# A two-layer hybrid trunk on one core: single returns of gated outputs, the place of one gate tile, and rotary tables one group later

## The chip, the cores and the metric

The kernel runs on one core of a Trainium2 chip, in one launch. The metric is the device time of that launch in microseconds (us). "Before" was run three times: 1938.21 us in the median (1937.47 to 1940.67). One further run carried the hardware profiler; its time and trace are what the text below reads.

In the profile PE is TensorE's matrix multiplications and PEld its weight loads, DVE is VectorE, ACT is ScalarE, POOL is GpSimd, and SP is SyncE, which in this kernel issues nearly all DMA transfers. L126 is line 126 of the kernel.

## The reference

A sequence of 512 positions of width 2048 passes two layers; everything is float32.

```python
def pool_mixer_layer(x, norm_g, w_in, w_group, scale, w_out):     # layer A
    h = rmsnorm(x, norm_g)
    proj = h @ w_in                                               # 2048 -> 2 * 4096
    u, gate = proj[..., :W_A], proj[..., W_A:]
    u = u.reshape(B, S, N_POOL_GROUPS, G_A)                       # 4 groups of 1024
    pooled = jnp.stack([causal_mean_pool(u[:, :, gi], w) - u[:, :, gi]
                        for gi, w in enumerate(POOL_WINDOWS)], axis=2)   # 2, 4, 8, 16
    y = jnp.einsum('bsgc,gcd->bsgd', pooled, w_group).reshape(B, S, W_A) * scale
    return x + (y * jax.nn.silu(gate)) @ w_out                    # 4096 -> 2048
...
# layer B: 16 heads; a key has 128 plain and 64 rotary columns, a value 128
k, v = shared_kv(x, ...)            # latent of 512 -> keys (QK-norm, rotary) and values
h = rmsnorm(x, norm_g)
proj = h @ w_in                     # q latent of 512, and 16 gate tiles of 128
q = qk_norm_rope(rmsnorm(latent) @ w_q_b, ...)
o = chunk_causal_attention(q, k, v) # query blocks of 128, mask by chunks of 64
x = x + (o * jax.nn.silu(gate)) @ w_out
```

The rotation uses cos and sin of position times frequency, tables that both keys and queries of layer B need.

## The kernel before, in words

**Products.** Activations stand with channels on the 128 partitions and the 512 positions along the row. For precision each operand is split in two parts, hi (a cast, on ACT) and lo (the rest, on DVE), and a product is three matmuls: hi·hi (L144), hi·lo (L145), lo·hi (L146), in `mm3`. `split` (L149) makes the two parts of an activation. `load_w` does the same for a weight tile: a DMA into `raw` (three buffers), the cast into `whi` (L126), the subtraction into `wlo` (L127) (four buffers each). `proj` walks over a weight in tiles of four 128-row slices, of 256 KB each.

**Layer A.** The in-projection (lines up to L412) leaves its 64 output tiles in DRAM. Then four groups g follow, one for each pooling window. In each, eight `y_tile`s fetch a gate tile z from DRAM (L453), multiply by the norm (L454), apply SiLU (L455), make the group product with weights `awg` and combine it with z (L458) and split it. Then 16 output products with weights `awo` follow, and with every second one of them the next group's `pooled_tile` loads a tile from DRAM and pools it (`pool_tile`, lines L232 to L259; its first step on DVE is L243, the window sums L250). `rope_tables` (L181 to L206, small DVE operations and two sines on ACT) stands in the code between the y tiles and the output products of group 0. `rope_gains` (L208 to L218), which multiplies the tables by the norm gains, is written further down, where they are used; the scheduler starts it early, behind the tables.

**Layer B, the gate tiles.** After the latents, `gate_unit` computes gate tiles 0 to 13 and stores each in DRAM (`gates`, named `gd` in the trace). Tiles 14 and 15 are made by `gate_part`, in four pieces of 12 matmuls each, within the first round of attention below.

**Attention.** The heads go in eight rounds hg of two heads. TensorE's order is written out by hand and pinned. A main sequence of 64 steps (hg, head h, query block i) issues scores (`score_unit`, L786; on DVE a memset L787, the maximum L789, its scaling L791), the exponential on ACT (`exp_unit`, L799), the scaling on DVE (`scale_unit`, L805 and L806), the transposition (`pt_unit`, L814, with splits L826 and L828) and the product with values (`pv_unit`, L844 to L846). Beside it a list `fill` of small pieces is used up between these steps by `fill_to`: a piece is a planned time, a weight tile, a function and its arguments. `prep_items(hg)` builds a round's pieces: k and v (`kv_part`, 16 pieces, L641 to L643), q (`q_part`, 16 pieces, L664 to L666), transpositions (`tr_unit`, L752) and statistics. The pieces of round 0 run ahead of the steps; those of a later round run between the steps of the round ahead of it, and the tail between those of round 7. `split_due` issues the load of a weight tile four tiles ahead of its use. Other engines than PE are ordered by a scheduler that takes the written order and a simulated time line.

**The return of the gated outputs.** A head's attention output is multiplied by its gate and stored in DRAM (L849, L852). For the last product, over 16 heads with weights `bwo`, it comes back: `og_load(h)` (L916) loads it into a buffer `at` (heads 0 to 7) or `bt` (8 to 13), `og_unit(h)` splits it there (L149). Heads 14 and 15 never leave the chip. `part(o, k0, n)` is a fill piece: n heads from k0 on, into output tile o, one `bwo` tile. The fill's end, `tail`, holds the parts of output tiles 0 to 2 for heads 0 to 13, with `ld` (loads) and `og` (splits) between. After the main sequence `out_unit` does the same for tiles 3 and 4 (`NO` is 3), then all five get heads 14 and 15, and the other eleven tiles follow whole; `out_store` (L936 to L940) adds the residual and stores.

Of the kernel before, what the change touches and what calls it, by code (L numbers as in the profile page):

```python
# [47 lines left out]
def trunk_kernel(  # L48
# [417 lines left out]
    for g in range(NG):  # L466
        ys = []
        for o in range(8):
            with ExitStack() as c5:
# [4 lines left out]
                ys.append(y_tile(g, o, pooled))  # L474
        if g == 0:
            rope_tables()
# [317 lines left out]
    def exp_unit(hg, h, i):  # L794
        n = (i + 1) * P
        s, nm, rq = st[hg][("P", h, i)]
        pe = tt_()
        sm = small(1, "sm", 4)
        A.activation(pe[:, 0:n], s[:, 0:n], AF.Exp, bias=nm, scale=rq, accum_out=sm)  # L799
        st[hg][("P", h, i)] = pe, sm  # L800

    def scale_unit(hg, h, i):
        pe, sm = st[hg][("P", h, i)]
        n = (i + 1) * P
        V.reciprocal(sm, sm)  # L805
        V.tensor_scalar(pe[:, 0:n], pe[:, 0:n], sm, None, ALU.mult)  # L806

# [46 lines left out]
    def prep_items(hg, nxt, mid=()):  # L854


        def piece(us, fn, *a, w=None):
            return us, w, fn, a
# [19 lines left out]
        first += mid  # L878
        if end:
            first += ld(0, 1, 2, 3)  # L880
        first += [q(0, 0), q(0, 1), kq(3), q(0, 2), q(0, 3)]
        if own:
            first += [piece(0, kstats_unit, hg)]
        first += [q(1, 0), q(1, 1), qq(0), q(1, 2), q(1, 3)]
        if own:
            first += [kr(0), tr_(0)]
        first += [q(2, 0), qq(1), q(2, 1)]
        if own:
            first += [kr(1)]
        if end:  # L890
            first += og(0)
        first += [q(2, 2), q(2, 3)]
        if own:
            first += [tr_(2, 0)]
        if end:
            first += og(1) + ld(4, 5)
        first += [q(3, 0), qq(2), q(3, 1)]
        if end:
            first += og(2) + ld(6, 7)
        first += [q(3, 2), q(3, 3)]  # L900
        if end:
            first += og(3)
        first += nxt[:1] + [qq(3)]
        if own:
# [63 lines left out]
    def ld(*hs):  # L968
        return [(0, None, og_load, (h,)) for h in hs]
# [7 lines left out]
    tail = (part(0, 0, 4) + part(1, 0, 4) + og(4, 5) + part(2, 0, 4) + og(6, 7) + ld(8, 9) + part(0, 4, 4) +  # L977
            ld(10, 11) + part(1, 4, 4) + og(8) + part(2, 4, 4) + og(9, 10) + ld(12, 13) + og(11) +
            part(0, 8, 4) + part(1, 8, 4) + og(12) + part(2, 8, 4) + og(13) +
            part(0, 12, 2) + part(1, 12, 2) + part(2, 12, 2))  # L980
# [71 lines left out]
    for m in range(len(seq) + 2):  # L1052
        now = seq[m] if m < len(seq) else None
        if now:
# [4 lines left out]
            score_unit(*now)  # L1059
            beside(hg, 4 * h + i, 0)  # L1060
        if m >= 2 and seq[m - 2][2] % 2:
            pv_unit(*seq[m - 2][:2], seq[m - 2][2] // 2)
        if now:
            fill_to(at_ + share * 0.35)
            exp_unit(*now)
        if 1 <= m <= len(seq):
            pt_unit(*seq[m - 1])
        if now:
# [3 lines left out]
            fill_to(at_ + share)  # L1072
    fill_to(c + 99)
    PINNED = (mybir.EngineType.PE,)
# [81 lines left out]
```

## Time and profile before

| | before |
|---|---|
| median of 3 runs | 1938.21 us (1937.47 to 1940.67) |
| profiled execution | 1935.33 us |
| its span in the trace | 1933.4 us |
| granted TensorE clock | 1.0 |
| PE busy | 1910.7 us, 99%, 11356 instructions |
| DVE busy | 1279.4 us, 66% |
| ACT busy | 806.7 us, 42% |
| POOL busy | 287.3 us, 15% |
| DMA | 251.26 MB, mean 130 GB/s |

The span runs from the first to the last instruction in the trace; the 1.9 us between it and the execution's time lie outside. The "chain that ended last" is followed back from the last instruction, at each step to what released it; a row of it has start, length (us) and what ran. "issue" in it is time for which the trace shows no cause. A row of waits names the engine and line that waited, the instruction that ended the wait, the total, the number of waits and the longest. In a row of a timeline stand start, length, engine, line, operation, output, inputs and shape, and in brackets the idle time before it with what ended it.

### The profile page before, as it was taken

How to read it: one execution, taken by the hardware profiler on the slowest of the kernel's cores; microseconds unless marked ns; L12 is line 12 of the kernel's file. 1: busy time of each engine (PE TensorE's matmuls, PEld its weight loads, DVE VectorE, ACT ScalarE, POOL GpSimd, SP SyncE). 2: the span in 40 equal slices, each digit the busy share in tenths (PEclk: the TensorE clock that was granted, in tenths of full speed). 3: DMA queues.
4: the chain of work that ended last, by engine and by line, in shares of the span. 5: the costliest groups of instructions: out<-in, count | busy, mean ns of one | idle time of the engine just before them, and what ended most of it. 6: DMA issues, size and time to landing. Idle time of an engine off the chain costs nothing.

```text
span 1933.4 us, 30664 instructions
## 1 busy us (share of the span) xinstructions
PE 1910.7 (99%) x11356; PEld 1704.1 (88%) x11356; DVE 1279.4 (66%) x2249; ACT 806.7 (42%) x1506; POOL 287.3 (15%) x436
## 2 busy tenths in 40 slices
PE   8999999999999999999999999999999999999999
PEld 8999999999999977888888888888888999988887
DVE  8677786797666677486595477474335888896332
ACT  8444333333333433233333354233235777774221
POOL 0433232343323100000000000000001332320000
PEclk9999999999999999999999999999999999999999
DMA  6555443434444446434344344233432222243642
GB/s 190 160 157 164 143 141 122 131 121 143 156 134 137 157 138 213 128 122 143 120 123 137 107 147 134 91 100 118 124 111 89 87 90 81 78 137 111 211 120 88
DMA packets 176646, 251.26 MB, mean 130 GB/s; under 512 B 15728, under 2 KB 95984, under 8 KB 176496
## 3 DMA queue, kind: packets, MB, share of 16 engines
q1 hardware_dynamic: 176208, 249.10, 41.1%
q8 instruction: 89, 1.46, 0.3%
q14 instruction: 61, 0.50, 0.1%
q10 hardware_dynamic: 288, 0.20, 0.0%
HBM read 216.21 MB, written 33.03 MB: 129 GB/s over the span
## 4 chain that ended last, share of the span: by engine, by line
PE 88%; DMA 4%; DVE 4%; issue 1%; ACT 1%; SPq 1%; POOL 0%; DVEq 0%; ACTq 0%; POOLq 0%
PE mm L146 15%; PE mm L144 14%; PE mm L145 14%; PE k L337 10%; PE k L335 10%; PE k L333 10%; PE sc L786 2%; PE mm L641 2%; PE mm L643 1%; PE mm L642 1%; PE mm L664 1%; PE mm L666 1%; PE mm L665 1%; PE tr L814 1%; PE tr L752 1%
## 5 line engine op out<-in xcount | busy, mean ns | idle before, releaser
L126 ACT CAST whi<-raw 128x512 fp32r<-128x512 f32 (+2 forms) x421 | 254.4, 609 | 515.7 <-PE mm L145 444.4
L333 PE MATMUL k<-xc,hi 128*128 128x256 f32 x1680 | 460.1, 283 | 0.1
L335 PE MATMUL k<-xc,hi 128*128 128x256 f32 x1680 | 460.0, 283 | 0.0
L127 DVE TENSOR_TENSOR wlo<-raw,whi 128x512 fp32r<-128x512 f32 (+2 forms) x421 | 285.0, 678 | 237.7 <-ACT whi L126 236.5
L337 PE MATMUL k<-xc,lo 128*128 128x256 f32 x1680 | 417.8, 283 | 1.1 <-DVE lo L315 1.0
L146 PE MATMUL mm<-bt,wlo 128*128 128x512 f32 x944 | 368.5, 391 | 1.7 <-DVE wlo L127 1.7
L144 PE MATMUL mm<-bt,whi 128*128 128x512 f32 x944 | 367.9, 390 | 0.9 <-ACT bt L149 0.9
L145 PE MATMUL mm<-bt,whi 128*128 128x512 f32 x944 | 367.2, 389 | 0.0
L314 ACT CAST hi<-raw 128x1792 fp32r<-128x1792 f32 x120 | 202.8, 1690 | 364.5 <-PE k L337 249.9
L315 DVE TENSOR_TENSOR lo<-raw,hi 128x1792 fp32r<-128x1792 f32 x120 | 248.4, 2070 | 158.9 <-ACT hi L314 158.7
L333 PEld LDWEIGHTS k<-xc,hi 128*128 128x128 f32 x1680 | 322.5, 192 | 0.3 <-ACT hi L314 0.3
L335 PEld LDWEIGHTS k<-xc,hi 128*128 128x128 f32 x1680 | 322.5, 192 | 0.0
L337 PEld LDWEIGHTS k<-xc,lo 128*128 128x128 f32 x1680 | 296.8, 192 | 2.2 <-DVE lo L315 1.7
L146 PEld LDWEIGHTS mm<-bt,wlo 128*128 128x128 f32 x944 | 177.2, 188 | 40.4 <-DVE wlo L127 3.1
L144 PEld LDWEIGHTS mm<-bt,whi 128*128 128x128 f32 x944 | 177.2, 188 | 38.0 <-ACT bt L149 1.3
L145 PEld LDWEIGHTS mm<-bt,whi 128*128 128x128 f32 x944 | 177.2, 188 | 37.0 <-DVE bt L149 0.2
L146 PE MATMUL mm<-at,wlo 128*128 128x512 f32 x432 | 168.6, 390 | 1.7 <-DVE wlo L127 1.7
L145 PE MATMUL mm<-at,whi 128*128 128x512 f32 x432 | 168.9, 391 | 0.2 <-DVE at L149 0.2
L144 PE MATMUL mm<-at,whi 128*128 128x512 f32 x432 | 168.5, 390 | 0.0
L310 POOL TENSOR_TENSOR raw<-raw 128x256 f32<-128x256 f32 x120 | 97.1, 809 | 434.4 <-DVE raw L308 412.2
L311 POOL TENSOR_TENSOR raw<-raw 128x256 f32<-128x256 f32 x120 | 105.7, 880 | 9.2
L146 PEld LDWEIGHTS mm<-at,wlo 128*128 128x128 f32 x432 | 81.1, 188 | 20.0 <-DVE wlo L127 3.2
(1151 smaller groups left out, 2541.7 us busy)
## 6 DMA issues: line engine op xcount, KB each, us to landing
raw<-awin SPq DMA_DIRECT2D x240, 256.0 KB, 3.2
raw<-awo SPq DMA_DIRECT2D x128, 256.0 KB, 2.9
raw<-bwin SPq DMA_DIRECT2D x80, 256.0 KB, 2.8
raw<-awg SPq DMA_DIRECT2D x64, 256.0 KB, 2.8
raw<-bwo SPq DMA_DIRECT2D x59, 256.0 KB, 2.8
scr<-e SPq DMA_DIRECT2D x56, 256.0 KB, 2.7
raw<-wkvb SPq DMA_DIRECT2D x32, 256.0 KB, 2.9
raw<-wqb SPq DMA_DIRECT2D x32, 192.0 KB, 2.4
```

Source lines behind the costliest of these rows:

```text
L126: A.copy(hi[:, :n], raw[:, :n])
L127: V.tensor_tensor(lo[:, :n], raw[:, :n], f(hi[:, :n]), ALU.subtract)
L144: T.matmul(dst, wh, xh, start=first, stop=False)
L145: T.matmul(dst, wh, xl, start=False, stop=False)
L146: T.matmul(dst, wl, xh, start=False, stop=last)
L310: G.tensor_tensor(c[:, :, 6, :], c[:, :, 4, :], c[:, :, 2, :], ALU.add)
L311: G.tensor_tensor(c[:, :, 7, :], c[:, :, 6, :], c[:, :, 3, :], ALU.add)
L314: A.copy(hi, c[:, :, 1:8, :])
L315: V.tensor_tensor(lo, c[:, :, 1:8, :], f(hi), ALU.subtract)
L333: T.matmul(dst, hi[:, j % 2, wi, :], xh[j][:, xi, :], start=first, stop=False, skip_group_check=True)
L335: T.matmul(dst, hi[:, j % 2, wi, :], xl[j][:, xi, :], start=False, stop=False, skip_group_check=True)
L337: T.matmul(dst, lo[:, j % 2, wi, :], xh[j][:, xi, :], start=False, stop=last, skip_group_check=True)
```

## The change

Five edits.

1. The rotary tables are written behind group 1's y tiles instead of group 0's.
2. Gate tile 15 leaves its place between kv and q of round 0 (gate 14 stays there). Its four pieces go behind q, ahead of round 1's kv, with round 0's last transpositions and the q statistics among and behind them.
3. Among round 7's pieces the gated outputs come back one at a time: `ld(0)` to `ld(3)` are spread over the q pieces. And `og_unit` gets an order: its cast on ACT stands behind the last exponential that is written ahead of it, its subtraction on DVE behind the last scaling.
4. In the tail the first four heads' parts are cut into two halves of two heads, with one `og` and one `ld` between each; loads and splits run some pieces ahead of their use.
5. Output tile 3's four products for heads 0 to 13 are written around the last scores and the last value products, inside the pinned order. Tile 4's stay behind.

```diff
-        if g == 0:
+        if g == 1:
             rope_tables()
...
-        A.activation(pe[:, 0:n], s[:, 0:n], AF.Exp, bias=nm, scale=rq, accum_out=sm)
+        st["exp"] = A.activation(pe[:, 0:n], s[:, 0:n], AF.Exp, bias=nm, scale=rq, accum_out=sm)
...
-        V.tensor_scalar(pe[:, 0:n], pe[:, 0:n], sm, None, ALU.mult)
+        st["scale"] = V.tensor_scalar(pe[:, 0:n], pe[:, 0:n], sm, None, ALU.mult)
...
-        if end:
-            first += ld(0, 1, 2, 3)
...
+        if end:
+            first += ld(0)
         first += [q(1, 0), q(1, 1), qq(0), q(1, 2), q(1, 3)]
...
+        if end:
+            first += ld(1)
         first += [q(2, 0), qq(1), q(2, 1)]
...
         if end:
-            first += og(0)
-        first += [q(2, 2), q(2, 3)]
+            first += og(0) + ld(2)
+        first += [q(2, 2), q(2, 3), q(3, 0), qq(2), q(3, 1)]
+        if end:
+            first += og(1) + ld(3)
+        first += [q(3, 2), q(3, 3)]
         if own:
-            first += [tr_(2, 0)]
...
-            return first + [piece(0, qstats_unit, hg), tr_(3)] + nxt[1:4] + [tr_(5)] + nxt[4:]
-        return first + nxt[1:]
+            return (first + nxt[:1] + [tr_(3)] + nxt[1:4] + [tr_(2, 0), qq(3), piece(0, qstats_unit, hg)] +
+                    nxt[4:5] + [tr_(5)] + nxt[5:])
+        return first + nxt[:1] + [qq(3)] + nxt[1:]
...
-        split(f(lo) if h < 14 else gated[h], hi, lo)
+
+        for ins, name in zip(split(f(lo) if h < 14 else gated[h], hi, lo), ("exp", "scale")):
+            if name in st:
+                tc.add_manual_dep(ins.ins, st[name].ins.name, mybir.DependencyInfo(
+                    mybir.DependencyClass.NoSync, mybir.DependencyReason.DATA), reason="softmax first")
...
-    tail = (part(0, 0, 4) + part(1, 0, 4) + og(4, 5) + part(2, 0, 4) + og(6, 7) + ld(8, 9) + part(0, 4, 4) +
...
+    tail = (part(0, 0, 2) + og(2) + ld(4) + part(1, 0, 2) + og(3) + ld(5) + part(2, 0, 2) + og(4) +
+            part(0, 2, 2) + ld(6) + og(5) + part(1, 2, 2) + ld(7) + og(6) + part(2, 2, 2) + ld(8, 9) + og(7) +
+            part(0, 4, 4) + og(8) + ld(10, 11) + og(9) + part(1, 4, 4) + og(10) + ld(12, 13) + og(11) +
+            part(2, 4, 4) + part(0, 8, 4) + og(12) + part(1, 8, 4) + og(13) + part(2, 8, 4) +
...
-    fill = prep_items(0, fill, gate_items(14) + gate_items(15))
+    fill = prep_items(0, gate_items(15) + fill, gate_items(14))
...
+        if m == len(seq) + 1:
+            out_unit(NO, 4, 4)
         if m >= 2 and seq[m - 2][2] % 2:
             pv_unit(*seq[m - 2][:2], seq[m - 2][2] // 2)
...
+        if m == len(seq):
+            fill_to(c + 99)
+            out_unit(NO, 0, 4)
...
-    fill_to(c + 99)
+    out_unit(NO, 8, 4)
+    out_unit(NO, 12, 2)
...
-    for o in range(NO, NO + 2):
-        for k0, n in ((0, 4), (4, 4), (8, 4), (12, 2)):
-            out_unit(o, k0, n)
+    for k0, n in ((0, 4), (4, 4), (8, 4), (12, 2)):
+        out_unit(NO + 1, k0, n)
```

How this stands in the engines' order, at three places. On ACT in round 6, where round 7's pieces stand between the steps, around head 12's second query block (tt__18109 is its exponential), before: three casts of gated outputs (`at<-at`) stand in a row, then one, then two more right behind an exponential (L799).

```order
L126 CAST whi<-raw 128x384
L149 CAST at<-at 128x512 x3
L149 CAST at<-mm 128x256
L826 CAST xt<-tr 128x128
L126 CAST whi<-raw 128x384
L149 CAST at<-at 128x512
L149 CAST bt<-tr 128x512
L799 ACTIVATE tt__18109,sm<-sc,nm,qy 128x256
L149 CAST at<-at 128x512 x2
```

On the same engine now, a little later in that round (tt__18246 and tt__18323 are exponentials of the next steps):

```order
L826 CAST xt<-tr 128x2x128
L826 CAST xt<-tr 128x128
L799 ACTIVATE tt__18246,sm<-sc,nm,qy 128x512
L149 CAST at<-at 128x512
L670 COPY qt<-mm 128x384
L126 CAST whi<-raw 128x256
L677 ACTIVATE junk,ssq<-qt 128x192 x2
L126 CAST whi<-raw 128x256
L826 CAST xt<-tr 128x2x128 x2
L799 ACTIVATE tt__18323,sm<-sc,nm,qy 128x128
L149 CAST at<-at 128x512
```

Each such cast stands alone, and behind an exponential. The weights' casts of 256 columns are those of the half parts.

On DVE, in group 1's output stage, the difference (a piece of it; tt__9144 is group 2's first pooled tile, tt__8012 a pooled tile of the same kind in group 0's output stage, qsin a table with gains):

```order
+L199 SCALAR_TENSOR_TENSOR tt__9043<-tt__9043 128x128 x2
+L200 SCALAR_TENSOR_TENSOR tt__9043<-tt__9043 128x128
 L127 TENSOR_TENSOR wlo<-raw,whi 128x512
 L204 SCALAR_TENSOR_TENSOR cn<-cn,sn 128x128
 L205 SCALAR_TENSOR_TENSOR sn<-sn 128x128
 L217 SCALAR_TENSOR_TENSOR qsin<-cn,cs 128x32
-L243 SCALAR_TENSOR_TENSOR tt__8012<-tt__8010,r 128x512
+L243 SCALAR_TENSOR_TENSOR tt__9144<-tt__9142,r 128x512
 L218 TENSOR_TENSOR qsin<-cn,cs 128x32
```

The tables stand around a pooled tile of group 1's output stage as they stood around one of group 0's.

On SP, in round 0 of the attention, the difference (bwin are gate weights, wqb those of q, wkvb those of kv; tt__14259 is gate tile 15):

```order
 L606 DMA gd<-tt__14055 128x512
-L125 DMA raw<-bwin 128x512 x5
+L125 DMA raw<-bwin 128x512
+L125 DMA raw<-wqb 128x384 x4
+L125 DMA raw<-bwin 128x512 x3
+L953 DMA gd<-tt__14259 128x512
+L125 DMA raw<-bwin 128x512
+L125 DMA raw<-wkvb 128x512 x4
 L125 DMA raw<-wqb 128x384 x3
-L954 DMA gd<-tt__14259 128x512
```

The gate's loads moved behind the four last tiles of wqb, and the next wkvb tiles behind the gate's.

More of the change, by code (lines that the diff above doesn't have):

```diff
@@ L890, in prep_items @@
         if end:
-            first += og(0)
-        first += [q(2, 2), q(2, 3)]
-        if own:
-            first += [tr_(2, 0)]
[L895 to L904, printed above, removed]
-            return first + [piece(0, qstats_unit, hg), tr_(3)] + nxt[1:4] + [tr_(5)] + nxt[4:]
-        return first + nxt[1:]
+            first += og(0) + ld(2)
[3 more added lines that the diff above has]
+        first += [q(3, 2), q(3, 3)]
+        if own:
+            return (first + nxt[:1] + [tr_(3)] + nxt[1:4] + [tr_(2, 0), qq(3), piece(0, qstats_unit, hg)] +
+                    nxt[4:5] + [tr_(5)] + nxt[5:])
+        return first + nxt[:1] + [qq(3)] + nxt[1:]
     ogs = [None] * NH
```

2 lines of the change are left out of this document (removed).

## The prediction

> **What bounds the kernel.** I read the page's first part, then TensorE's waits, then the windows around each longest wait.
>
> ```profile
> span 1933.4 us, 30664 instructions
> PE 1910.7 (99%) x11356; PEld 1704.1 (88%) x11356; DVE 1279.4 (66%) x2249; ACT 806.7 (42%) x1506; POOL 287.3 (15%) x436
> ```
>
> TensorE works 1910.7 of 1933.4 us and the change keeps its instructions. Only its idle 22.7 us can be won, less what the start and the end take. Which waits are in it (line, releaser, us, times, longest):
>
> ```profile
> PE mm L146 <- DVE wlo L127: 3.5, 4, 1.4
> PE tr L814 <- DVE tt__18804 L806: 2.7, 1, 2.7
> PE tr L814 <- DVE tt__18109 L806: 2.4, 1, 2.4
> PE mm L641 <- ACT whi L126: 1.4, 1, 1.4
> PE mm L144 <- ACT bt L149: 0.9, 1, 0.9
> ```
>
> The change touches these five rows, 10.9 us. By window (PE, loads, DVE, ACT, POOL, clock, DMA share, GB/s):
>
> ```profile
> 1450.00:1500.00 50.00, 48.51 (x241) 41.02 (x240) 26.86 (x76) 28.53 (x84) 8.44 (x20) 1.00 0.30 90
> 1700.00:1750.00 50.00, 47.55 (x290) 41.94 (x289) 44.35 (x136) 36.15 (x106) 12.33 (x20) 1.00 0.44 140
> 1750.00:1800.00 50.00, 47.22 (x249) 40.02 (x248) 28.19 (x74) 20.98 (x50) 0.00 (x0) 1.00 0.43 136
> 1800.00:1850.00 50.00, 50.00 (x223) 41.38 (x222) 18.61 (x29) 12.43 (x21) 0.00 (x0) 1.00 0.56 176
> ```
>
> Each of the first three loses 1.5 to 2.8 us, nearly all in one wait. The last, only products of 512 columns, loses none; there a matmul costs 50.00 / 223 = 0.224 us, my unit for cover.
>
> **Gated outputs and the tail.** The chain of waits into the two longest stops:
>
> ```profile
> 1711.39 5.58 DMA at<-gd
> 1716.99 0.63 ACT at L149
> 1717.64 0.69 DVE at L149
> 1718.33 0.27 DVE tt__18109 L806
> 1718.74 0.41 PE tr L814 x2
> ...
> 1759.96 3.96 DMA bt<-gd
> 1763.99 0.48 issue
> 1764.47 0.87 ACT tt__18804 L799 x2
> 1765.66 0.43 DVE wlo L127
> 1766.09 0.41 DVE tt__18804 L806
> 1766.63 0.41 PE tr L814 x2
> ```
>
> In both, a gated output on its way back from DRAM (at or bt) is split on ScalarE and VectorE ahead of softmax work that was ready. In the first, DVE takes two splits ahead of the scaling L806; in the second ACT has waited 2.06 us on the load before it may do the exponential:
>
> ```profile
> 1716.99 1.34 DVE L149 TENSOR_TENSOR at<-at 128x512 fp32r<-128x512 f32 x2 [0.25 <-ACT at L149]
> 1763.27 1.29 ACT L149 CAST bt<-bt 128x512 fp32r<-128x512 f32 x2 [2.06 <-DMA bt<-gd]
> ```
>
> The change loads one output at a time and puts each split's cast behind the last exponential written and its subtraction behind the last scaling. The two stops go: −2.4 − 2.7 = −5.1. What is late next?
>
> (a) The first use of an output. Half parts of products now stand just behind its load and split. A load at this place and its weights:
>
> ```profile
> at<-gd SPq DMA_DIRECT2D x8, 256.0 KB, 4.9
> bt<-gd SPq DMA_DIRECT2D x11, 256.0 KB, 4.1
> raw<-bwo SPq DMA_DIRECT2D x15, 256.0 KB, 3.0
> raw<-bwo SPq DMA_DIRECT2D x10, 128.0 KB, 2.3
> ```
>
> The 4.9 is of loads issued four in a row; alone I expect nearer the 3.0 of one weight tile. Cast 0.63 and subtraction 0.69 follow: 3.0 + 0.63 + 0.69 = 4.3 us from issue to use. Pieces of k or q products lie between the first loads and their splits; the first part of each weight slice needs only older outputs, 6 matmuls, 1.3 us. Covered, except at one place, the second half of part (0, 0) (output 1), where ACT has an exponential and three casts before it. From 0 (the later parts run behind full rounds of scores) to 2.4 (the same wait as now); I take 0.9, nearer the covered end, since only ACT's order is in question.
>
> (b) The softmax itself. One transposition now follows its scores with one product part between; maximum, exponential and scaling must fit beneath it. From 0 to 2.74 (a whole stop again); in the trace an exponential of 128 columns waited 1.28 for VectorE's maximum, so I take 1.1, nearer that than a stop:
>
> ```profile
> 1766.91 0.46 ACT L799 ACTIVATE tt__18849<-sc,nm,qy 128x128 f32<-128x128 f32 x1 [1.28 <-DVE nm L791]
> ```
>
> The added order has the same cost from the other side: where the last exponential waits like this one, the split's cast waits behind it, and behind that on ACT the weight casts. A split so delayed is needed only by a first use, so the price is that of (a), not another. No instruction moves on POOL's queue.
>
> (c) Six half parts for three whole ones make three more weight DMAs, casts and subtractions, of half the size. A half subtraction took 0.43 (the chain), so two half ones cost some 0.2 more than the 0.68 of a whole one: 3 × 0.2 on a DVE that is 89% busy in 1700 to 1750 and 56% after. Weights are loaded four tiles ahead of their products, and that hides it: 0. If that cover went, the loads themselves would show, rival four.
>
> (d) The products for o = 3 around the last scores: before, they stood behind and between them, and TensorE has no gap after 1766.63 either way, so moving the cover is worth 0 (a gain only inside −5.1). What still stands behind, o = 4 and the products of heads 14 and 15, is some 60 matmuls, 13 us, longer than the 4.3 us of the last splits.
>
> The tail: −5.1 + 0.9 + 1.1 = −3.1, between −5.1 and 0.
>
> [...]
>
> **Gate 15 behind q.** Between q and kv the fourth weight of kv comes late:
>
> ```profile
> 1483.53 2.97 DMA raw<-wkvb
> 1486.58 0.63 ACT whi L126
> 1487.25 0.50 PE mm L641
> ```
>
> TensorE waits 1.4 us at L641. The change takes gate 15's four pieces, 48 matmuls or 48 × 0.224 = 10.8 us, from ahead of q to behind it, so the kv weights get 10.8 us more from q's last weight on. That exceeds the whole path 2.97 + 0.63 + 0.69 = 4.3, so the wait goes (−1.4). The gate's own weights then come behind q's four on SP; q's products run longer than their loads, and the row of 3.0 us per 256 KB under 2.7 us of products (12 × 0.224) bounds a new wait at 4 × 0.3 = 1.2 us; buffers four ahead take that, so 0 is nearer. The gate's store and the later load of output 15 lie hundreds of us apart. The q statistics move behind the kv pieces; they feed scores that stand later, with 4 × 2.7 us more beside them: 0. Small gains beside it (transpositions out of the way): −0.1. Sum −1.5, between −2.2 and 0.
>
> **Rotary tables.** They leave group 0's output stage for group 1's. On DVE, before, at the stop of 700:
>
> ```profile
> 696.99 0.69 DVE L243 SCALAR_TENSOR_TENSOR tt__8012<-tt__8010,r 128x512 f32<-128x512 f32 x1 [1.09 <-DMA tt__8010<-scr]
> 698.45 0.75 DVE L458 SCALAR_TENSOR_TENSOR tt__7719<-mm,cs,tt__7719 128x512 f32<-128x512 f32 x1
> 699.71 0.68 DVE L127 TENSOR_TENSOR wlo<-raw,whi 128x512 fp32r<-128x512 f32 x1
> ...
> 700.45 0.50 PE L146 MATMUL mm<-at,wlo 128*128 128x512 f32 x1 [1.33 <-DVE wlo L127]
> 715.24 0.50 PE L144 MATMUL mm<-bt,whi 128*128 128x512 f32 x1 [0.90 <-ACT bt L149]
> 761.18 0.50 PE L146 MATMUL mm<-bt,wlo 128*128 128x512 f32 x1 [1.41 <-DVE wlo L127]
> ```
>
> VectorE waited 1.09 us for a pooled tile, the tables' little operations stood behind that wait, and the low half of a weight came 1.33 late. Without them group 0 loses that 1.33 and, by the same relief, half of the 0.90 at 715 (0.4). The 1.41 at 761 has no table work near it and stays. The order shows the same tables in the same neighbourhood in group 1, ahead of the same kind of pooled tile, so the stop can come back there: 0 if that tile's load is earlier, 1.33 if the same, up to 2 × 1.33 if that group is tighter (its pooling window is wider: one more addition per tile). I take 0.9, nearer 1.33 than 0. Sum −1.33 − 0.4 + 0.9 = −0.8, between −1.7 and +1.3.
>
> **The sum.** −3.1 − 1.5 − 0.8 = −5.4. Against its own execution, 1935.33 us (span 1933.4 and 1.9 around it), 1929.9. That execution lies 2.88 below the median of 1938.21; carried over, 1932.8. All ends together: −5.1 − 2.2 − 1.7 = −9.0 (1929.2) to +1.3 (1939.5).
>
> **The rivals.**
>
> *One: singles come late every time (slower).* A load alone exposes its whole latency: the path of 4.3 us, of which only part is covered, at each of the five first uses (outputs 0 and 1, 2 and 3, 4 to 7, 8 to 11, 12 and 13). For it speak 5.58 us for the load in the chain; against it, that SP queue wait was four loads deep, and the order leaves rounds of scores between. At 2.4 each, +12, less 5.1 + 1.5 + 0.8 won: 1938.2 + 4.6 = 1942.8. It decides from (7.4 + 3.9) / 5 = 2.3 us per first use.
>
> *Two: the rotary stop moves and doubles.* In group 1 it costs 2 × 1.33 and group 0 keeps its 0.90: −1.33 + 2.66 = +1.3, so −3.1 − 1.5 + 1.3 = −3.3, 1934.9. For it speaks the equal neighbourhood; against it, 1.09 of the stop came from one late load.
>
> *Three: loads wait for their places.* SP has waited for a place of a gated output, until TensorE was past L643:
>
> ```profile
> SPq L916 <- PE mm L643: 12.1, 2, 11.7
> ```
>
> If singles wait for places as the fours did, or a store of the last head has to be awaited, one of the two stops stays, 2.4 to 2.7: −5.4 + 2.7 = −2.7, 1935.5. Against it: a place for one is free sooner than for four.
>
> *Four: small loads show their fixed cost.* The six half loads come end to end, each 2.3 us over 1.3 us of products: +6 × 1.0 = 6.0, less 5.4: 1938.8, no change. Against it: weights are issued four ahead; the 1800 to 1850 window at 176 GB/s has no gap.
>
> *Five: nothing is done.* The order shows that it does move instructions, on ACT, DVE and SP; I give it no chance of its own.
>
> **How the numbers follow.** No change means within 0.2% of 1938.21, 3.9 us: 1934.3 to 1942.1, about what three runs can tell. Forecast 0.60; one 0.05; two 0.16; three 0.13; four 0.06. The likeliest is 1932.8, its own range 1929.2 to 1936. Leaving about 2 in 10 out, one and four fall outside, and below 1929 little: range 1928.8 to 1937.6. Faster: most of the forecast (0.56 of 0.60), a third of two (0.06) and a third of three (0.04): 0.66. Same: the rest of these (0.04 + 0.10 + 0.09), four, and one just under its deciding point (0.01): 0.30. Slower: 0.04.
>
> **What would show it.** Right: the rows L814 <- L806 at 1718 and 1766 and L641 <- whi gone; loads of at at about 3 us, each alone on SP; windows 1700 to 1800 at 49 or more busy; a smaller wait on wlo L127 in group 0 and one of up to 1.3 among the rows of group 1. Wrong: new rows of L144 <- ACT at or bt L149 (first uses, rival one), L814 <- L806 under other names (term b), L643 still ahead of the loads (three), L144 <- whi L126 in the tail (four), wlo L127 growing beyond 3.5 us (two). If the windows 1700 to 1800 stay at 47.5, the tail term failed and the time is about 1936.

## The result, and the profile after

The changed kernel takes 1923.21 us (median of 6, 1922.54 to 1924.31); the kernel before, on the same chip, 1937.84 (median of 6). The ratio is 0.9924, interval 0.9912 to 0.9937: 14.6 us less, where 5.4 less was forecast. It lies below the range.

The page's first part, after:

```profile
span 1921.5 us, 30674 instructions
PE 1906.1 (99%) x11356; PEld 1704.7 (89%) x11356; DVE 1278.6 (67%) x2252; ACT 807.1 (42%) x1509; POOL 280.9 (15%) x436
```

TensorE's longest waits, after:

```profile
PE k L386 <- ACT hi L149: 6.2, 1, 6.2
PE k L337 <- DVE lo L315: 2.2, 3, 1.7
PE tr L814 <- DVE tt__18582 L806: 1.2, 1, 1.2
PE mm L145 <- DVE at L149: 1.0, 2, 0.8
PE tr L814 <- DVE tt__14821 L806: 0.8, 1, 0.8
```

The first two lie in the in-projection and are no part of the change. Of the five rows that the prediction listed, none is left. In their place stand two: a first use of a gated output (L145, 0.8 of the 1.0) and one late softmax step (tt__18582, 1.2).

The stretches, in two fences: the kernel before, then after. Columns: PE, PEld, DVE, ACT and POOL busy, clock, DMA share, GB/s.

```profile
650.00:780.00 130.00, 125.40 (x586) 102.20 (x585) 95.37 (x181) 50.80 (x87) 0.90 (x8) 1.00 0.56 178
780.00:900.00 120.00, 120.00 (x531) 99.38 (x530) 84.68 (x138) 40.76 (x69) 0.90 (x8) 1.00 0.43 134
```

```profile
650.00:780.00 130.00, 129.76 (x615) 108.14 (x615) 93.29 (x151) 52.23 (x88) 0.89 (x8) 1.00 0.58 186
780.00:900.00 120.00, 120.00 (x531) 99.41 (x530) 89.18 (x172) 41.75 (x71) 0.89 (x8) 1.00 0.42 133
1700.00:1750.00 50.00, 48.03 (x290) 43.04 (x289) 46.32 (x139) 36.69 (x105) 10.04 (x20) 1.00 0.53 165
1750.00:1800.00 50.00, 50.00 (x254) 42.45 (x253) 26.45 (x65) 17.48 (x42) 0.00 (x0) 1.00 0.48 156
```

From 650 to 780, group 0, TensorE starts 615 matmuls instead of 586. 29 × 0.224 = 6.5 us (an estimate, by the prediction's time of one matmul) is the largest gain in the trace, in the part for which 0.8 was forecast. From 780 to 900, which holds the tables now, VectorE does 4.5 us more and TensorE loses nothing. In the tail 1750 to 1800 is full, and 1700 to 1750 still loses 2.0 (48.03 busy, under the 49 that the prediction named as a sign of being right).

In the profiled executions the gain is 12.0 us (1935.33 against 1923.34), in the medians 14.6. The difference lies in the granted clock of the kernel before, as the experiments on the tail below show.

### The profile page after: what moved, and what is told of

Its sections match the earlier page's. It is cut to its first block, busy times and chain, and to the rows that moved or that the text cites. A ratio compares the mean times of both kernels' runs of the same rounds, so it can differ in the third digit from the quotient of the medians.

```text
span 1921.5 us, 30674 instructions
## 1 busy us (share of the span) xinstructions
PE 1906.1 (99%) x11356; PEld 1704.7 (89%) x11356; DVE 1278.6 (67%) x2252; ACT 807.1 (42%) x1509; POOL 280.9 (15%) x436
## 4 chain that ended last, share of the span: by engine, by line
PE 94%; DVE 3%; DMA 1%; issue 1%; ACT 0%; SPq 0%; POOL 0%; DVEq 0%; POOLq 0%; ACTq 0%
PE mm L145 16%; PE mm L146 16%; PE mm L144 16%; PE k L337 10%; PE k L335 10%; PE k L333 10%; PE sc L786 3%; PE mm L641 2%; PE mm L643 2%; PE mm L642 2%; PE mm L664 1%; PE mm L666 1%; PE mm L665 1%; PE tr L814 1%; PE tr L752 1%; DMA raw<-awin 1%
## 5 line engine op out<-in xcount | busy, mean ns | idle before, releaser
L127 DVE TENSOR_TENSOR wlo<-raw,whi 128x512 fp32r<-128x512 f32 (+2 forms) x424 | 285.7, 675 | 235.7 <-ACT whi L126 232.6
L146 PE MATMUL mm<-bt,wlo 128*128 128x512 f32 x944 | 368.1, 390 | 0.0
L144 PE MATMUL mm<-bt,whi 128*128 128x512 f32 x944 | 367.7, 390 | 0.0
L145 PE MATMUL mm<-bt,whi 128*128 128x512 f32 x944 | 367.2, 389 | 0.0
L314 ACT CAST hi<-raw 128x1792 fp32r<-128x1792 f32 x120 | 202.8, 1690 | 364.9 <-PE k L337 249.6
L146 PEld LDWEIGHTS mm<-bt,wlo 128*128 128x128 f32 x944 | 177.2, 188 | 37.5 <-DVE wlo L127 0.5
L144 PEld LDWEIGHTS mm<-bt,whi 128*128 128x128 f32 x944 | 177.2, 188 | 36.9 <-ACT whi L126 0.2
L145 PEld LDWEIGHTS mm<-bt,whi 128*128 128x128 f32 x944 | 177.3, 188 | 36.8
L145 PE MATMUL mm<-at,whi 128*128 128x512 f32 x432 | 169.0, 391 | 1.0 <-DVE at L149 1.0
L144 PE MATMUL mm<-at,whi 128*128 128x512 f32 x432 | 168.8, 391 | 0.0
L146 PE MATMUL mm<-at,wlo 128*128 128x512 f32 x432 | 168.2, 389 | 0.0
L310 POOL TENSOR_TENSOR raw<-raw 128x256 f32<-128x256 f32 x120 | 98.6, 821 | 439.9 <-DVE raw L308 422.1
L311 POOL TENSOR_TENSOR raw<-raw 128x256 f32<-128x256 f32 x120 | 99.1, 826 | 9.2
L145 PEld LDWEIGHTS mm<-at,whi 128*128 128x128 f32 x432 | 81.1, 188 | 19.2 <-DVE at L149 2.6
```

Source lines behind the costliest of these rows:

```text
L127: V.tensor_tensor(lo[:, :n], raw[:, :n], f(hi[:, :n]), ALU.subtract)
L144: T.matmul(dst, wh, xh, start=first, stop=False)
L145: T.matmul(dst, wh, xl, start=False, stop=False)
L146: T.matmul(dst, wl, xh, start=False, stop=last)
L310: G.tensor_tensor(c[:, :, 6, :], c[:, :, 4, :], c[:, :, 2, :], ALU.add)
L311: G.tensor_tensor(c[:, :, 7, :], c[:, :, 6, :], c[:, :, 3, :], ALU.add)
```

## The experiments

Each was timed in five rounds or more beside the kernel before. Times within 2 us on different chips are not told apart here; the intervals are those of the ratio to the kernel before on the same chip. "Over the changed kernel" compares medians taken on different chips, so traces are read beside them.

### The tables: buffer, work or place?

Two theories of why the tables' place is worth so much. "Buffer": their scratch tile takes one of six and delays the pooled tiles. "Work": their VectorE operations delay the low halves of weights. e1 puts the tables back:

```diff
-        if g == 1:
+        if g == 0:
             rope_tables()
```

> The changed kernel with the rotary tables back in group 0; all else as changed (1923.2 us). Both theories, buffer and work: the waits on wlo L127 and bt L149 between 687 and 762 us come back, +5 to +8 us, 1928 to 1931. If the tables' place is worth only the 0.8 us of the prediction: 1924.0.

Measured 1927.30 (ratio 0.9945, 0.9933 to 0.9958): 4.1 over the changed kernel, less than the 5 to 8 expected and far more than 0.8. TensorE's waits of that kernel between 640 and 800 us:

```profile
PE mm L146 <- DVE wlo L127: 3.1, 3, 1.7
PE mm L144 <- ACT bt L149: 0.8, 1, 0.8
```

e2 keeps that and takes the scratch from another pool:

```diff
-        buf = tt_()[:, 0:256].rearrange("p (a t d) -> p a t d", a=2, t=4)
+        buf = bt(dt=F32)[:, 0:256].rearrange("p (a t d) -> p a t d", a=2, t=4)
```

> The tables in group 0 as in the run above, but their scratch tile comes from the pool of y parts (32 places, half free) and not from the six scratch tiles of layer A. Theory 'buffer': the scratch tile took one of six places, so the first pooled tile's load stood behind two more weight loads on SP and all pooled tiles ran late; with its own place the load stands where the changed kernel has it, and the time is the changed kernel's within 1 us, 1923 to 1925. Theory 'work': the 40 or so small VectorE operations of the tables are what comes in the way; the time stays at that of the run above, +5 to +8, 1928 to 1931.

1924.39 (0.9930, 0.9918 to 0.9943), as "buffer" has it. But the trace shows that the scheduler had also moved the work. One of the tables' operations, in a row of its line (count, ns min/median/max, first and last start):

```profile
L199 DVE SCALAR_TENSOR_TENSOR bt<-bt x6: 282/285/293, 718.6 to 727.3; 128x128 f32<-128x128 f32 x6
```

In e1 the tables run from 689 to 701, in e2 from 714 to 736, 25 to 35 us later. So e2 changed two things and does not decide between the two theories. But it shows that this work is not dear everywhere in group 0: there it cost TensorE nothing, though VectorE was nearly full (e2; columns as above):

```profile
714.00:737.00 23.00, 23.00 (x104) 19.02 (x103) 22.04 (x66) 7.22 (x13) 0.35 (x3) 1.00 0.58 178
```

e3 holds the tile without the work:

```diff
+        if g == 0:
+            held = tt_()
+            V.memset(held[:, 0:1], 0.0)
+            V.tensor_tensor(held[:, 0:1], held[:, 0:1], f(ys[5][0])[:, 0:1], ALU.add)
```

> The changed kernel, tables in group 1, and in group 0 only one of the six scratch tiles held (two VectorE operations on one column, the second behind y tile 5) as long as the tables held it. Theory 'buffer': the waits between 687 and 762 come back without any table work, +4 to +8, 1927 to 1931. Theory 'work': nothing, 1923.2 within 1.

1922.71 (0.9920, 0.9907 to 0.9934). The held tile costs nothing, and "buffer" falls. Then the work without the tables, in group 0 (e11) and in group 1 (e12):

```diff
+        if g == 0:          # e12: g == 1, behind the tables
+            extra = tt_()
+            V.memset(extra[:, 0:P], 1.0)
+            for _ in range(24):
+                V.scalar_tensor_tensor(extra[:, 0:P], extra[:, 0:P], 0.5, extra[:, 0:P], ALU.mult, ALU.mult)
```

> The changed kernel (tables in group 1) with 24 chained VectorE operations of 128 columns, some 7 us, used by nothing, written where the tables stood in group 0. Theory 'lead' (the low halves of weights are ready only 0.1 to 4 us ahead of their products there): +3 to +6, 1926 to 1929, waits on wlo L127 between 690 and 770. Theory 'the tables' own neighbourhood' (a load, a held tile): 0 to +1.

> The changed kernel with the same 24 chained VectorE operations, some 7 us, used by nothing, written behind the tables in group 1, so that group 1 carries twice the extra work that group 0 had before. Theory 'lead' (low halves are ready 7 us ahead of their products there, the tables took 2.6 of it): 1923.2 within 0.7. Theory 'the same neighbourhood, the same price' (as the prediction took it): +1 to +4, 1924 to 1927.

e11 took 1925.86 (0.9947, 0.9934 to 0.9959), e12 1923.24 (0.9930, 0.9918 to 0.9943); the changed kernel beside them (e9) 1922.86. So the same 24 operations cost 3.0 us in group 0, at 688 to 702 where the tables stood in e1, and 0.4, which is no difference here, in group 1. Waits between 640 and 800 in e11, then between 640 and 900 in e12:

```profile
PE mm L146 <- DVE wlo L127: 1.2, 2, 1.1
PE mm L144 <- ACT bt L149: 0.8, 1, 0.8
```

```profile
PE mm L145 <- DVE at L149: 0.2, 1, 0.2
```

In e12 the operations did run in group 1, among the tables and behind them:

```profile
L480 DVE SCALAR_TENSOR_TENSOR tt__9066<-tt__9066 x24: 280/284/292, 818.9 to 844.2; 128x128 f32<-128x128 f32 x24
```

The lead offers a reason. TensorE uses the low halves of weights in the order in which VectorE makes them, four L146 to one L127. So the n-th L127 can be set against the first L146 that uses it, and the distance is the lead. At the stop of 700 in the kernel before it was nothing (the low half ready at 700.39, used at 700.45). In the changed kernel the tables cut deepest into group 1's lead at this pair:

```profile
824.15 0.69 DVE L127 TENSOR_TENSOR wlo<-raw,whi 128x512 fp32r<-128x512 f32 x1
...
829.32 0.39 PE L146 MATMUL mm<-at,wlo 128*128 128x512 f32 x1
```

Ready at 824.84, used at 829.32: 4.5 us of lead, with the tables beside it. Without tables there (the kernel before, same weight) the same count gives 7.1. In group 0 of the changed kernel it starts at 3.5 to 7.4 for the first four weights, falls to 0.6 at 674 and stays between 0.1 and 4.6 up to 761. From 689 to 701, where the tables stood, the kernel before has 0.05 to 1.0. In e2 it is 0.7 to 3.0 while the tables run, and they are spread over 22 us instead of 12. So what counts is that place, not the group.

The delay also reaches far behind. The four kernels of this page with the tables in their old place (before, e1, e13, e15) all have a wait of L146 at 759 to 761, 0.7 to 1.8 us long, and no other kernel has one there. In e11 the lead falls to 0.05 there, where the changed kernel has 1.5, without such a wait. The waits agree with a lead that was lost and not won back; in the kernel before VectorE had also waited 1.93 us for a load just ahead of that stop, and how much of it is the load's is not settled.

### The gate

```diff
-    fill = prep_items(0, gate_items(15) + fill, gate_items(14))
+    fill = prep_items(0, fill, gate_items(14) + gate_items(15))
...
-            return (first + nxt[:1] + [tr_(3)] + nxt[1:4] + [tr_(2, 0), qq(3), piece(0, qstats_unit, hg)] +
-                    nxt[4:5] + [tr_(5)] + nxt[5:])
+            return first + nxt[:1] + [qq(3), piece(0, qstats_unit, hg), tr_(3)] + nxt[1:4] + [tr_(5)] + nxt[4:]
```

> The changed kernel with gate tile 15 back between kv and q, and the transpositions and q statistics back in their places. As predicted: the wait of 1.4 us of L641 on whi comes back and little else, +1.5, 1924.7 (1923.2 to 1925.4). Rival: the place of the gate also set other waits at the start of the attention, +3 or more, 1926 up.

1927.13 (0.9945, 0.9932 to 0.9957), 3.9 over the changed kernel, with the expected row back (1400 to 1520):

```profile
PE mm L641 <- ACT whi L126: 1.6, 1, 1.6
PE tr L814 <- DVE tt__14821 L806: 0.9, 1, 0.9
```

The other way round, edit 2 alone on the kernel before:

> The kernel before with gate tile 15 behind q (and the transpositions and statistics that go with it) and nothing else. By the prediction's term: -1.5, 1936; by the traces (2.3 us less between the first kv product and the 40th score): -2.3, 1935; by the take-back: -3.9, 1934.

1936.56 against 1936.96 beside it (0.9993, 0.9982 to 1.0004): 1.4 less by the ratio, 0.4 by the medians, not told from nothing. The times leave 0 to 3.9 us; the traces are sharper. From the first kv product (L641) to the first score of round 0's second head TensorE runs the same number of instructions in every kernel. The kernel before takes 67.5 us for them (1440.9 to 1508.4) and e15 65.2 (1438.4 to 1503.6); e4 takes 67.8 (1436.0 to 1503.8) and the changed kernel 65.2 (1435.1 to 1500.3). So the gate is worth 2.3 to 2.6 us both ways, and the rest of e4's 3.9 lies outside the stretch that the edit touches. Beside the wait at L641 two waits of TensorE's weight loads went, which the list of PE's waits does not show (the kernel before, 1434 to 1509):

```profile
PEld mm L643 <- DVE wlo L127: 1.0, 2, 0.6
```

### The tail

e5 takes edits 3 to 5 back together:

```diff
-    tail = (part(0, 0, 2) + og(2) + ld(4) + part(1, 0, 2) + og(3) + ld(5) + ...
+    tail = (part(0, 0, 4) + part(1, 0, 4) + og(4, 5) + part(2, 0, 4) + og(6, 7) + ld(8, 9) + ...
...
+        split(f(lo) if h < 14 else gated[h], hi, lo)
...
+        if end:
+            first += ld(0, 1, 2, 3)
...
+    for o in range(NO, NO + 2):
+        for k0, n in ((0, 4), (4, 4), (8, 4), (12, 2)):
+            out_unit(o, k0, n)
```

> The changed kernel (1923.2 us) with edits 3, 4 and 5 taken back: loads in fours and twos, splits free, whole parts, output tile 3 behind the main sequence; tables and gate as changed. As predicted the tail is worth 3.1 us: 1926.3; by where the scores stand in the two traces (last score 3.9 us earlier over that stretch) 1927.1. Rival: the two stops are all there is and nothing came in their place, 5.1: 1928.3. Rival: the tail gave nothing and all came from gate and tables, 1923.2.

1931.42 (0.9977, 0.9967 to 0.9986): 8.2 over the changed kernel (10 by the two ratios), beyond every theory. Its waits, 1690 to 1800:

```profile
PE tr L814 <- DVE tt__18109 L806: 2.6, 1, 2.6
PE tr L814 <- DVE tt__18804 L806: 2.4, 1, 2.4
PE mm L664 <- ACT whi L126: 0.5, 1, 0.5
PE tr L752 <- DVE xt L828: 0.4, 1, 0.4
PE tr L814 <- DVE qa L162: 0.3, 1, 0.3
```

The two stops sum to 5.0, against 2.0 for the two waits after. That is near the 3.1 of the prediction. But the clock, the third figure from the end in a row of a window, is not 1.00 here. Windows of e5, then TensorE's rows behind the first stop:

```profile
1710.00:1720.00 10.00, 7.47 (x39) 7.16 (x40) 8.52 (x30) 5.70 (x21) 4.62 (x10) 0.83 0.34 129
1712.00:1716.00 4.00, 3.47 (x15) 3.41 (x16) 3.55 (x19) 2.50 (x13) 1.60 (x4) 0.58 0.35 135
1760.00:1770.00 10.00, 7.58 (x39) 6.52 (x39) 5.47 (x17) 3.98 (x12) 0.00 (x0) 0.83 0.13 37
```

```profile
1712.53 0.66 PE L814 MATMUL tr<-cs,tt__18109 128*128 128x128 f32 x2 [2.64 <-DVE tt__18109 L806]
1713.31 0.52 PE L665 MATMUL mm<-whi,at 128*128 128x384 f32 x1
1713.63 0.52 PE L666 MATMUL mm<-wlo,at 128*128 128x384 f32 x1
1713.95 0.52 PE L664 MATMUL mm<-whi,at 128*128 128x384 f32 x1
...
1715.74 0.33 PE L665 MATMUL mm<-whi,at 128*128 128x384 f32 x1
1715.91 0.33 PE L666 MATMUL mm<-wlo,at 128*128 128x384 f32 x1
```

Behind the stop a product of 384 columns starts every 0.32 us; from 1715.7 on, every 0.17. The starts, almost twice as far apart, put the clock there near half. At half, 10 us at 0.83 hold 3.4 us of it (0.17 × 10 / 0.5), and so do the 4 us at 0.58 (0.42 × 4 / 0.5); that costs up to 1.7 us at each stop (an estimate from these windows: the length times a half).

Whether it happens differs from run to run. Over 62 runs of the kernel before on four chips, by mean granted clock:

| granted clock | runs | mean us |
|---|---|---|
| 1.0 | 8 | 1934.2 |
| 0.999 | 26 | 1936.0 |
| 0.998 | 15 | 1938.2 |
| 0.997 | 12 | 1939.2 |
| 0.996 | 1 | 1942.8 |

The mean is rounded, and the end of the launch counts in it: e7's profiled execution stands at 0.999 although every window of 10 us up to 1920, in the last of which its matmuls end (9.40 us busy), shows 1.00; the trace of the kernel before, whose last matmul starts at 1929.3, shows 0.79 from 1932.0 to 1933.4. All 11 runs of the changed kernel (with e9) are at 1.0. The profiled execution of the kernel before was at 1.0 too, so it showed none of this. Two kernels test it. They put work into the stops, used by nothing: in e10 on the kernel of e5, in e13 on the kernel before.

```diff
         p = tr()
+        if (hg, h, i) in ((6, 0, 1), (7, 0, 3)):
+            v0 = d["vh"][0][:, 0, :]
+            for _ in range(16):
+                T.matmul(p[:, 0:256], v0[:, 0:P], v0[:, 0:256], start=True, stop=True)
         for j in range(i + 1):
             T.transpose
```

> The kernel with the old tail (tables and gate as changed; 1931.4 us, granted clock 0.997 to 0.999) with 16 matmuls of 256 columns added ahead of each of the two transpositions at which it stops. They write what the transpositions overwrite and are used by nothing; 16 of them take about 1.9 us, less than the stops of 2.4 and 2.6. Theory 'clock': the stops let the granted clock fall to half for 3.4 us each, 1.7 us lost in each; with the added work it stays at 1.0 and the time falls by 1.5 to 3.5, to 1928 to 1930, though more work is done. Theory 'stops alone': the same stops, half filled; the time stays within 0.5 of 1931.4 or rises by up to 1.

> The kernel before with 16 matmuls of 256 columns (some 1.9 us, used by nothing) ahead of each of the two transpositions at which its tail stops. Theory 'clock': its runs sit at a granted clock of 0.997 to 0.999, half clock for 3.4 us behind a stop, and its profiled run at 1.0 was one of the few without; with the added work all runs are at 1.0 and the median falls by 2 to 4, to 1933 to 1935. Theory 'stops alone': no change within 1, or up to 1 slower.

e10 took 1927.28 (0.9950, 0.9937 to 0.9964), all five runs at 1.0: 4.1 less than e5, with 32 matmuls more, and a little more than the 1.5 to 3.5 expected. e13 took 1934.79 beside 1936.96 (0.9986, 0.9977 to 0.9995): 2.2 less by the medians, 9 of 11 runs at 1.0, where 4 of 27 of the kernel before are. Their windows at the first stop, e10 and then e13:

```profile
1710.00:1720.00 10.00, 9.73 (x65) 9.20 (x64) 9.38 (x35) 8.27 (x30) 7.20 (x13) 1.00 0.25 94
```

```profile
1710.00:1720.00 10.00, 9.20 (x59) 8.19 (x58) 9.02 (x27) 7.95 (x25) 1.52 (x4) 1.00 0.87 299
```

The clock theory stands; 2 to 4 us of the median lay in it.

The traces agree. From the first score of round 0's second head to the end the changed kernel takes 421.2 us (1500.3 to 1921.5). The kernel before, with the clock at 1.00 in every window of 50 us from 1500 to 1900, takes 425.0 (1508.4 to 1933.4), e5 with its two stretches at half clock 429.8 (1501.3 to 1931.1), and e10 425.0 again (1500.3 to 1925.3). So the tail's edits are worth 3.8 us at full clock. e5 is 4.8 longer than the kernel before: 3.4 is the estimate for the two stretches, and 1.2 are its three small waits (L664, L752 and the one on qa), which the kernel before does not have in its trace.

Why only some stops are hit they do not show. The length of the stop does not tell it: e14 has stops of 2.5 us at tt__18109 and of 2.8 at tt__18804, and the clock is lower only behind the second. Its windows at the two:

```profile
1710.00:1720.00 10.00, 6.84 (x40) 5.81 (x39) 8.56 (x29) 8.28 (x26) 1.52 (x4) 1.00 0.77 253
1760.00:1770.00 10.00, 7.16 (x30) 5.77 (x29) 5.97 (x18) 3.44 (x10) 0.00 (x0) 0.83 0.30 103
```

In e15 the stops are 2.4 and 2.5 us, and both windows of 20 us with them are at 0.91; the kernel before has 2.4 and 2.7, and its windows of 10 us from 1690 to 1780 stay at 1.00. TensorE's busy time in 10 us does not tell it either: 6.84 at 1.00 in e14, and 7.60 and 7.26 at 1.00 in the kernel before, beside 7.47 and 7.58 at 0.83 in e5. No run was made to find what does.

Then single edits of the tail, each undone in the changed kernel. e6: `split(...)` alone in place of the loop with the added order.

> The changed kernel without the order of the splits behind the last exponential and scaling; single loads, halves and the place of tile 3 stay. Theory 'order': the splits get ahead of ready softmax work again, +2 to +5, 1925 to 1928. Theory 'singles': a load that comes back alone is there when its split is due, and the order adds little, 0 to +0.5, 1923.2 to 1923.7.

1925.74 (0.9944, 0.9931 to 0.9958), 2.5 over, with its runs at 1.0. Its longest wait in the tail:

```profile
PE tr L814 <- DVE tt__18158 L806: 1.5, 1, 1.5
```

The stretch to the end is longer by about as much (423.6 against 421.2). The wait is of the same kind as the two stops of before, but shorter. That a single load holds up less, and that the order removes the rest, fits this and was not tested further.

e7, the products of output tile 3 back behind the sequence:

> The changed kernel with output tile 3's products all behind the main sequence. As predicted they only change places with other cover: 1923.2 within 0.5. Rival: around the last scores they are the only cover for the last softmax steps (maximum, exponential and scaling of 512 columns, some 2.5 us each), +2 to +5, 1925 to 1928.

1925.14 (0.9942, 0.9928 to 0.9955), 1.9 over and not told from the changed kernel, whose interval it overlaps. Its trace has the same two waits in the tail, 1.2 and 0.8. The scores by their operands, the second head of round 0 (xt) and the later ones (count, ns min/median/max, first and last start, shapes), of the changed kernel and then of e7:

```profile
L786 PE MATMUL sc<-bt x300: 220/333/421, 1484.5 to 1765.9; 128*128 128x128 f32 x45, 128*128 128x384 f32 x45, 128*128 128x256 f32 x30, 128*128 128x512 f32 x30
...
L786 PE MATMUL sc<-xt,bt x4: 275/312/393, 1500.3 to 1515.3; 128*128 128x128 f32 x1, 128*128 128x256 f32 x1, 128*128 128x384 f32 x1, 128*128 128x512 f32 x1
```

```profile
L786 PE MATMUL sc<-bt x300: 220/333/421, 1486.3 to 1767.7; 128*128 128x128 f32 x45, 128*128 128x384 f32 x45, 128*128 128x256 f32 x30, 128*128 128x512 f32 x30
...
L786 PE MATMUL sc<-xt,bt x4: 275/312/393, 1502.2 to 1517.1; 128*128 128x128 f32 x1, 128*128 128x256 f32 x1, 128*128 128x384 f32 x1, 128*128 128x512 f32 x1
```

From the second head's first score to the last one it is 265.6 and 265.5 us, and to the end 421.2 in both: nothing, as predicted. The 1.9 us lie ahead of all that the edit touches.

e8, whole parts:

```diff
-    tail = (part(0, 0, 2) + og(2) + ld(4) + part(1, 0, 2) + og(3) + ld(5) + part(2, 0, 2) + og(4) +
...
+    tail = (og(2) + ld(4) + og(3) + ld(5) + part(0, 0, 4) + og(4) + ld(6) + og(5) + part(1, 0, 4) + ld(7) + og(6) +
```

> The changed kernel with the first four heads' parts whole (four heads, one weight tile of 256 KB each) behind the splits of the first four outputs, loads and splits single as changed. Theory 'halves matter': output 2 and 3's splits stand ahead of the first part and TensorE waits for them, +1 to +3, 1924.2 to 1926.2. Theory 'halves are free of effect': 1923.2 within 0.5; if the first wait on at L149 (0.8 us in the changed kernel's trace) goes with the larger weight tile, 1922.5.

1926.55 (0.9951, 0.9936 to 0.9967), 3.3 over; the stretch to the end takes 424.5, again 3.3 more. TensorE stops once in the tail, and the mean clock is below 1.0 in three of five runs:

```profile
PE tr L735 <- DVE bt L149: 2.6, 1, 2.6
```

So this order with whole parts is dearer, though by a transposition that waits and not by the first use: two subtractions of gated outputs (L149) stand ahead of it on VectorE again. e8 also puts the splits closer together, so the size of the parts alone was not tested.

e16, output 1's split earlier:

```diff
-        first += [q(2, 2), q(2, 3), q(3, 0), qq(2), q(3, 1)]
+        first += [q(2, 2), q(2, 3), q(3, 0)]
         if end:
             first += og(1) + ld(3)
-        first += [q(3, 2), q(3, 3)]
+        first += [qq(2), q(3, 1), q(3, 2), q(3, 3)]
```

> The changed kernel with output 1's split two pieces of q (1.1 us) earlier. If the wait of 0.8 us at L145 on at L149 is the price of its late split alone: that row goes, -0.5 to -0.8, 1922.3 (too little to be told in the times, so by the trace). Rival: the cast then stands ahead of softmax or weight casts on ACT and another wait takes its place, 0 to +2.

1925.69 (0.9935, 0.9922 to 0.9947), no better; the stretch to the end takes 420.8 against 421.2. The wait at the first use is gone, another came:

```profile
PE tr L814 <- DVE tt__18582 L806: 1.3, 1, 1.3
PE tr L752 <- DVE nm L791: 0.6, 1, 0.6
```

### Do the parts add up?

The changed kernel again, and edit 1 alone on the kernel before:

> The changed kernel again, beside the three kernels below on one chip. 1923 to 1925, mean granted clock 1.0 in every run; the kernel before beside it at 0.997 to 1.0, with its runs at 0.998 some 3 to 4 us over those at 1.0.

> The kernel before with the rotary tables in group 1 and nothing else changed. By the take-back (4.1) and the traces (6.3 us less between 658 and 820): -4 to -6.5, 1931 to 1934, with the granted clock still below 1.0. By the prediction's term: -0.8, 1937.

e9: 1922.86 (0.9927, 0.9914 to 0.9939). e14: 1933.95 beside 1936.96 (0.9977, 0.9968 to 0.9986), 0.23% of 1937 or 4.5 us, as the take-back of 4.1 has it; no run is at 1.0, which fits, since the tail's stops are still there. By these times tables 4.1 to 4.5, gate 1.4 to 3.9, tail 8.2: 13.7 to 16.6, around the 14.6. No version tried is told from the changed kernel on the fast side.

The traces can be cut at the same three instructions: the first group product (L144), the first kv product (L641) and the first score of round 0's second head (us; the last column has one edit, or edits 3 to 5, taken back):

| stretch, and what lies in it | before | after | taken back |
|---|---|---|---|
| group product to kv product: tables | 779.8 | 773.5 | 779.2 (e1) |
| kv product to second head: gate | 67.5 | 65.2 | 67.8 (e4) |
| second head to the end: tail | 425.0 | 421.2 | 429.8 (e5) |

Between before and after that is 6.3, 2.3 and 3.8, together 12.4; the in-projection ahead of it took 0.5 longer in the trace of after, which leaves the 11.9 between the spans. One trace is not exact: the four kernels with the tables in their old place take 777.5 to 779.8 for the first stretch, the twelve with them in group 1 773.5 to 776.4 (e2 takes 773.8, e11 777.2). In the mean the tables are worth 4.7, near the 4.1 to 4.5 of the times. What the medians gain beyond the traces, 2.7, is the half clock that the trace of before happened not to have.

## Why the prediction was wrong

**Tables: −0.8 forecast, −4.1 to −4.5 measured.** Two steps failed. "so the stop can come back there" priced group 1 from the likeness of its VectorE order. The likeness held: VectorE waits for the pooled tile there too (1.02 us at 821). What was not read was the lead of the low halves, 7 us there and 0.05 to 1.0 where the tables stood. And "The 1.41 at 761 has no table work near it and stays" took waits as local; it went, here and in every other kernel without the tables in their old place. The rows of waits that the prediction had before it sum to 4.4 in group 0 (3.5 and 0.9); it let 1.7 of them go and put 0.9 back. They are no ceiling either: the stretch became 6.3 shorter in the profiled runs, and TensorE's busy time fell from 1910.7 to 1906.1 with the same instructions, so "Only its idle 22.7 us can be won" read the busy time too strictly.

**Tail: −3.1 forecast, 8.2 by the take-back.** The stops are right to a tenth: 5.1 became 2.0, with (a) 0.8 for 0.9 and (b) 1.2 for 1.1. That both terms came so near is partly luck: each was picked between 0 and a whole stop. The softmax did wait, as (b) says, but not for the length of its own steps: a weight's subtraction and the splits of transpositions stood ahead of it on VectorE. At full clock the tail gives 3.8 by the traces. What was missing is the clock at a stop. The failed step is "That execution lies 2.88 below the median of 1938.21; carried over, 1932.8": the difference was carried over as if it were no part of the change, though most of it was the cost of stops that the change removes. At 1.0, the kernel before takes 1934.2 in the mean. The two stretches at half clock, with three small waits, are 4.8 us in e5, and 3.8 + 4.8 is about the 8.2.

**Tail (c), (d).** The halves' extra loads cost nothing that a wait shows, (d) is 0 by e7's trace. The loads landed in 3.3 to 3.7 us against the 3.0 taken:

```profile
bt<-gd SPq DMA_DIRECT2D x10, 256.0 KB, 3.3
at<-gd SPq DMA_DIRECT2D x8, 256.0 KB, 3.7
raw<-bwo SPq DMA_DIRECT2D x16, 128.0 KB, 2.6
```

**Gate: −1.5 forecast, −2.3 to −2.6 by the traces.** The mechanism is right: the row L641 went as said. The term was too small, because two waits of the weight loads of L643 on their low halves, 1.0 together, went with it; it took 0.1 for everything beside the row.

**Rivals.** None came. Singles were late once, by 0.8. The tables' stop neither doubled nor moved. SP still waited 11.7 us for a place, now at L911, and no wait of TensorE followed from it:

```profile
SPq L911 <- PE mm L643: 12.7, 2, 11.7
```

No run separates a fixed cost of a small load, as rival four names it, from its bytes: the half tiles of 128 KB landed in 2.6 us, against the 2.3 taken, and in the trace after no wait of TensorE from 1690 to 1850 is on a weight.

## What to carry to other kernels

Before moving work to another place, read there how far ahead of its use each helper engine finishes, not only what stands beside it: here 24 operations cost nothing at a lead of 7 us and 3.0 us at a lead near 0, and the tables' delay showed up again 60 us behind. Read the very place: 25 us further on in the same group the tables cost nothing. Compare the granted clock of the profiled run with that of the timed ones: here the profiled run stood at 1.0 and 8 of 62 timed ones did, and in e5 stops of 2.6 and 2.4 us cost, by the estimate above, up to 1.7 us each beyond their length. To see what one edit gives, cut the traces at instructions that both kernels have in the same order and compare the stretches; here that was sharper than the times. An experiment that changes a buffer may move the scheduled work as well; look where it went before reading the time.

## What was not expected of the hardware

In some traces TensorE's clock was lower behind a stop of 2.4 to 2.8 us, and in others not. In e5 it was 0.83 over the 10 us around each of its two (2.6 and 2.4 us) and 0.58 in the window 1712 to 1716, with starts 0.32 apart for 0.17; by the estimate above that is 3.4 us at half clock each time. In e14 it was 1.00 around a stop of 2.5 and 0.83 around one of 2.8. The kernel before has both stops, 2.4 and 2.7 us, and its profiled execution has neither stretch, while over its runs the mean clock went from 1.0 to 0.996 and the time from 1934.2 in the mean to 1942.8. With 16 useless matmuls in each stop (2.07 us in e13's trace) the medians fell: e10's is 4.1 below e5's, e13's 2.2 below that of the kernel before. What sets the stops apart was not shown, nor how short a stop must be to leave the clock at 1.0: e7 and e16, whose longest waits in the tail are 1.2 and 1.3 us in their traces, each had one run at 0.998.
